# Where the operand tiles of the matmuls begin in on-chip memory, modulo 512 bytes: a two-layer decoder trunk in float32

## The chip, the core and the metric

The kernel runs on one core of a Trainium2 chip. The metric is the time of one execution on the device in microseconds (us). The kernel before took 2269.24 us in the median of three runs (2264.16 to 2272.15).

## What is computed

The reference is a decoder trunk on 256 tokens of width 2048, two layers deep, in float32, with a final RMSNorm. Cut to what matters here:

```python
h = x
# layer 0: one projection 2048 -> 6432, a gated short convolution and RWKV-7 mixing, one projection back
p = rms_norm(h, ev_norm) @ ev_w_in
mix = concat(short_conv_mixer(p[..., :3072], conv_w), rwkv7_mixer(p[..., 3072:], ...))
h = h + mix @ ev_w_out
h = h + (silu(n @ wg) * (n @ wu)) @ wd          # n = rms_norm(h, ffn_norm[0]), wg/wu 2048 x 5632
# layer 1: one projection 2048 -> 1600, a pooling mixer and 12-head latent attention, one projection back
p = rms_norm(h, od_norm) @ od_w_in
mix = concat(pool_mixer(p[..., :512], ...), mla_mixer(p[..., 512:], ...))
h = h + mix @ od_w_out
h = h + (silu(n @ wg) * (n @ wu)) @ wd          # the same block with the second set of weights
return rms_norm(h, final_norm)
```

Almost all arithmetic is in dense products of activations (256 tokens) with weights that are read once from device memory.

## The kernel before

Every dense product is done with three matmuls in a reduced float32 format (`float32r`): each operand is split into a high part and a low remainder, and high times high, high times low and low times high are summed in PSUM. Weights come in blocks of [128, 1024] through a queue of four buffers `w` (`load_next`, L67); `split_next` (L88) makes of each half a high tile `wh` (ScalarE, L96) and a low tile `wl` (VectorE, L97), [128, 512] each, six buffers of each, up to four ahead of use. One `wh` with its `wl` is a "quarter". All matmuls of the program pass through `mm` (L56), so they carry line 57 in the profile and are told apart by the names of their tiles. A name reads out <- moving operand, stationary operand: in `mm<-wh,xh` the weights stream and the activations stand.

There are two shapes of dense product. In `gemm_wt` the weights stand still (128 columns of a quarter) and 256 columns of activations stream past them. In `gemm_tok` the activations stand (128 tokens) and 512 columns of weights stream past them:

```python
# gemm_wt, L164-170: out[128 features, 256 tokens]
hi, lo = self.quarter()
for j in range(4):
    xh, xl = X[kt]
    self.mm(out, hi[:, sl], xh, kt == 0, False)
    self.mm(out, hi[:, sl], xl, False, False)
    self.mm(out, lo[:, sl], xh, False, kt == 4 * n - 1)
# gemm_tok, L181-187: out[t][128 tokens, 512 features]
for t in range(2):
    self.mm(out[t], xh[:, ts], hi, new and i == 0, False)
    self.mm(out[t], xl[:, ts], hi, False, False)
for t in range(2):
    self.mm(out[t], xh[:, ts], lo, False, stop and i == len(kts) - 1)
```

The activations are, by stage: `xh`/`xl` from `xtiles` (L141), four tiles of 4096 bytes a partition for the high and four for the low parts, used for the normed input of every projection, for the mixers' outputs in both output projections (`out_proj`, L237) and for the input of the feed-forward stages; `lh0`/`ll0` and `lh1`/`ll1` (L1108, named `lh`/`ll` in the profile), the two latents of the attention, used in `keys`, `queries` and `rotated` with `gemm_wt` and in `values` with `gemm_tok`; and `hh`/`hl` (L427), the gated hidden activations of a feed-forward stage, used in its down projections with `gemm_tok`.

The order of the stages is: the even layer's projections (`gemm_wt`, with the small matmuls of the recurrence woven between them by a list of generators, the "lane"), its output projection, feed-forward stage 0 in two halves (gate and up products of 6 blocks of 512, then the down products of these; then 5 blocks), the odd layer in the same manner, feed-forward stage 1. Nothing of this order is decided by addresses.

Where a tile begins in on-chip memory follows from the pools, which stand one behind another in every partition: `const`, then `xs` (small tiles and `xtiles`), then `wp` (`w`, `wh`, `wl`), then the pool of the running stage (`even`, `ff0`, `odd`, `ff1`). Within a pool, buffers stand in the order in which their tags are first asked for; sizes are rounded up to 32 bytes a partition. In `build`, line 305 asks for the small tags `dg`, `ssq` and `rstd` once before anything else of `xs`, and so they stand ahead of `xh` and `xl`.

Of the kernel before, what the change touches and what calls it, by code (L numbers as in the profile page):

```python
# [10 lines left out]
F32 = mybir.dt.float32  # L11
# [7 lines left out]
P = 128  # L19
# [32 lines left out]
class Trunk:  # L52
# [205 lines left out]
    def order(self):  # L258
        a, b = self.a, []
        for i in range(4):  # L260
            b.append([a["e_in"][n][:, i * 512 : i * 512 + 512] for n in range(4)])
        b += [a["e_in"][n] for n in range(4, 51)]

        def out(w, n0):
            r = [w[nb, kc] for nb in (2, 3) for kc in range(n0)]
            r += [w[nb, kc] for nb in (0, 1) for kc in range(3)]
            r += [w[nb, 3] for nb in (0, 1)]
            return r + [w[nb, kc] for nb in (2, 3) for kc in range(n0, 4)]

        def ffn(l):  # L270
            r = []
            for b0, b1 in HALVES:
                for n in range(b0, b1):
                    r += [a["f_gate"][l, n, kc] for kc in range(4)]
                    r += [a["f_up"][l, n, kc] for kc in range(4)]
                r += [a["f_down"][l, nb, kc] for nb in range(4) for kc in range(b0, b1)]
            return r

        b += out(a["e_out"], 3) + ffn(0)
        b += [a["o_in"][n] for n in range(13)]  # L280
        b += [a["w_v"][0], a["w_qp0"], a["w_kn"][0], a["w_qn"][0]]
        b += [a["w_kn"][1], a["w_qn"][1], a["w_v"][1], a["w_qp1"]]
        b += [a["w_kn"][2], a["w_qn"][2], a["w_v"][2]]
        return b + out(a["o_out"], 2) + ffn(1)

    def build(self):
        tc, nc, a = self.tc, self.nc, self.a
        self.ahead, self.half = 3, 0
        self.blocks, self.loaded, self.pend = self.order(), [], []
        self.delayed, self.lane, self.wait = [], [], 0  # L290
        with (
            tc.tile_pool(name="const", bufs=1) as cp,
            tc.tile_pool(name="xs", bufs=4) as self.xs,
            tc.tile_pool(name="wp", bufs=2) as self.wp,
            tc.tile_pool(name="psum", bufs=4, space=PSUM) as self.psum,
            tc.tile_pool(name="dram", bufs=2, space=bass.MemoryType.DRAM) as self.dp,
        ):
            self.ident = cp.tile([P, P], F32, name="ident")
            self.ones = cp.tile([P, P], F32, name="ones")
            self.pkt = cp.tile([P, NPK], F32, name="pkt")  # L300
            self.mhalf = cp.tile([P, 16], F32, name="mhalf")
            self.cos = cp.tile([P, T], F32, name="cos")
            self.sin = cp.tile([P, T], F32, name="sin")
            self.h = cp.tile([P, 2, D], F32, name="h")
            for tag, shape in (("dg", [P, P]), ("ssq", [P, 2, 4]), ("rstd", [P, 2])):
                self.xs.tile(shape, F32, tag=tag, name=tag, bufs=2)
            nc.vector.memset(self.mhalf, -0.5)
            nc.vector.memset(self.ones, 1.0)
            nc.scalar.dma_start(out=self.pkt, in_=a["pk"])
            nc.scalar.activation(self.cos[:, 0:16], self.mhalf, AF.Copy)  # L310
            with tc.tile_pool(name="even", bufs=1) as self.tp:
                X, ssq = self.even_mix()
            with tc.tile_pool(name="ff0", bufs=1) as self.tp:
                X, ssq = self.ffn(X, ssq, "g_od", self.rope_tables)
                rs = self.rstd_tok(ssq)
            with tc.tile_pool(name="odd", bufs=1) as self.tp:
                X, ssq = self.odd_mix(X, rs)
            with tc.tile_pool(name="ff1", bufs=1) as self.tp:
                self.fn = self.tp.tile([P, D], F32, tag="fn", name="fn")
                nc.gpsimd.dma_start(out=self.fn, in_=a["final_norm"].partition_broadcast(P))  # L320
                self.ffn(X, ssq, None)
# [82 lines left out]
    def ffn(self, X, ssq, gname, between=None):  # L404
        nc = self.nc
        rs = self.rstd_tok(ssq)
        new_ssq = self.xs.tile([P, 2, 4], F32, tag="ssq", name="ssq", bufs=2)
        for half, (b0, b1) in enumerate(HALVES):
            HX = []
            if half and between:  # L410
                between()
            for b in range(b0, b1):
                pg = self.gemm_tok(X, range(4))
                sg, ac = [], []
                for t in range(2):
                    s = self.tp.tile([P, 512], F32, tag="sg", name="sg", bufs=2)
                    nc.scalar.activation(s, pg[t], AF.Silu, scale=rs[:, t : t + 1])
                    sg.append(s)
                pu = self.gemm_tok(X, range(4))
                for t in range(2):  # L420
                    s = self.tp.tile([P, 512], F32, tag="ac", name="ac", bufs=2)
                    nc.vector.scalar_tensor_tensor(
                        out=s, in0=pu[t], scalar=rs[:, t : t + 1], in1=sg[t],
                        op0=ALU.mult, op1=ALU.mult,
                    )
                    ac.append(s)
                hh = self.tp.tile([P, 4, T], F32R, tag="hh", name="hh", bufs=6)  # L427
                hl = self.tp.tile([P, 4, T], F32R, tag="hl", name="hl", bufs=6)
                HX += [(hh[:, j], hl[:, j]) for j in range(4)]

                def turn(ac=ac, hh=hh, hl=hl):
                    for j in range(0, 4, 2):
                        pt = self.ps()
                        for i in range(2):
                            for t in range(2):
                                nc.tensor.transpose(  # L436
                                    pt[:, i * T + t * P : i * T + t * P + P],
                                    ac[t][:, (j + i) * P : (j + i + 1) * P], self.ident,
                                )
                        self.split(  # L440
                            (hh[:, j : j + 2], hl[:, j : j + 2]),
                            pt.rearrange("p (a t) -> p a t", a=2),
                        )

                self.later(3, turn)
            X = self.xtiles() if half and gname else X
            for nb in range(4):
                if half and not gname and nb == 3:
                    self.last(HX, b1 - b0, new_ssq)
                    break  # L450
                ps = self.gemm_tok(HX, range(b1 - b0))
                if not half:
                    self.add_h(ps, nb)
                elif gname:
                    self.finish(ps, nb, new_ssq, X, gname)
                else:
                    self.add_h(ps, nb, new_ssq)
                    hs = self.h[:, :, nb * 512 : nb * 512 + 512]
                    fs = self.fn[:, nb * 512 : nb * 512 + 512]
                    nc.vector.tensor_tensor(  # L460
                        out=hs, in0=hs, in1=fs.unsqueeze(1).to_broadcast([P, 2, 512]),
                        op=ALU.mult,
                    )
        return X, new_ssq
# [970 lines left out]
```

## Time and profile before

| | |
|---|---|
| median of 3 runs | 2269.24 us |
| the profiled execution | 2269.03 us |
| its span, first to last instruction | 2267.3 us |
| TensorE busy | 2250.6 us (99%) |
| VectorE busy | 1371.0 us (60%) |
| ScalarE busy | 1166.4 us (51%) |
| DMA, mean share of 16 engines | about a half, 179 GB/s |
| granted TensorE clock, mean | 0.997 of 2.4 GHz |

Time between the first and the last instruction is the span; 1.7 us of the execution lie around it. A matmul's busy time in the profile reaches from its start to the modelled end of its pipeline, so that the busy times of neighbours overlap: one of 512 columns stands as 389 ns, while the next one starts some 227 ns after it. What a matmul takes of the span is therefore read from the distance of two starts, which the text calls its step, and not from its duration. A window's count takes in the one or two matmuls that began before it and reach into it.

### The profile page before, as it was taken

What the parts mean: (1) busy time and instruction counts of PE and PEld (TensorE: products, weight loads), DVE (VectorE), ACT (ScalarE), POOL (GpSimd) and SP (SyncE); (2) the same over time, 40 slices, a digit from 0 to 9 for tenths busy, and PEclk for the clock granted to TensorE, in tenths of its full rate; (3) what the DMA queues carried; (4) which work ended last, traced back from release to release, by engine and by line L of the source; (5) the groups of instructions that cost most, each with busy time, mean ns of one, the idle gap of its engine ahead of it and who ended that gap; (6) DMA issues with size and microseconds to landing.
All of it is one profiled execution on the core that took longest, in us unless ns stands there. A gap on an engine that the chain in (4) does not pass through costs nothing.

```text
span 2267.3 us, 33957 instructions
## 1 busy us (share of the span) xinstructions
PE 2250.6 (99%) x12422; PEld 1921.0 (85%) x12422; DVE 1371.0 (60%) x2432; ACT 1166.4 (51%) x2085; POOL 27.1 (1%) x41
## 2 busy tenths in 40 slices
PE   9999999999999999999999999999999999999998
PEld 9999898778888888888888998788888888888886
DVE  6785477648555555555556677665555555555554
ACT  7655364546545444454555544455545444454554
POOL 0000000000000000000000000000000000000000
PEclk9999999999999999999999999999999999999999
DMA  8455235625555555555555554356555555555554
GB/s 300 134 177 166 85 132 171 196 88 185 189 191 190 192 188 194 194 187 193 188 189 190 178 171 136 117 178 208 186 194 187 189 193 193 195 187 192 188 190 154
DMA packets 124680, 405.46 MB, mean 179 GB/s; under 512 B 24896, under 2 KB 25152, under 8 KB 124128
## 3 DMA queue, kind: packets, MB, share of 16 engines
q1 hardware_dynamic: 122896, 398.31, 52.5%
q0 software_dynamic: 896, 3.80, 0.6%
q8 instruction: 97, 1.59, 0.3%
q10 hardware_dynamic: 720, 1.18, 0.1%
q14 instruction: 71, 0.58, 0.1%
HBM read 400.10 MB, written 3.15 MB: 178 GB/s over the span
## 4 chain that ended last, share of the span: by engine, by line
PE 96%; DMA 2%; DVE 1%; ACT 1%; issue 0%; SPq 0%; POOL 0%; POOLq 0%; DVEq 0%; ACTq 0%
PE mm L57 87%; PE sm L57 6%; PE sm L436 1%; DVE wl L97 1%; DMA xt<-x 0%; PE sm L198 0%; DMA Nb<-dN 0%; DMA xr<-xT 0%; DMA dN<-DG 0%; DMA pkt<-pk 0%; PE sm L1241 0%; ACT wh L96 0%; PE sm L700 0%; ACT xh L154 0%; PE sm L743 0%
## 5 line engine op out<-in xcount | busy, mean ns | idle before, releaser
L97 DVE TENSOR_TENSOR wl<-w,wh 128x512 fp32r<-128x512 f32 x1482 | 1017.3, 691 | 764.6 <-ACT wh L96 750.6
L96 ACT ACTIVATE wh<-w 128x512 fp32r<-128x512 f32 x1482 | 931.4, 631 | 952.1 <-DVE wl L97 630.1
L57 PE MATMUL mm<-wh,xh 128*128 128x512 f32 x1664 | 654.4, 393 | 2.2 <-ACT xh L151 2.2
L57 PE MATMUL mm<-wh,xl 128*128 128x512 f32 x1664 | 649.4, 390 | 1.2 <-DVE xl L152 1.2
L57 PE MATMUL mm<-wl,xh 128*128 128x512 f32 x1664 | 513.7, 390 | 0.0
L57 PEld LDWEIGHTS mm<-wh,xh 128*128 128x128 f32 x1664 | 312.9, 188 | 68.5 <-ACT xh L151 2.7
L57 PEld LDWEIGHTS mm<-wh,xl 128*128 128x128 f32 x1664 | 313.2, 188 | 64.8 <-DVE xl L152 1.5
L57 PEld LDWEIGHTS mm<-wl,xh 128*128 128x128 f32 x1664 | 312.6, 188 | 65.3
L57 PE MATMUL mm<-xh,wh 128*128 128x256 f32 x992 | 288.5, 291 | 1.3 <-ACT wh L96 1.3
L57 PE MATMUL mm<-xh,wl 128*128 128x256 f32 x992 | 282.4, 285 | 1.3 <-DVE wl L97 1.3
L57 PE MATMUL mm<-xl,wh 128*128 128x256 f32 x992 | 282.1, 284 | 0.0
L57 PE MATMUL mm<-wh,hh 128*128 128x512 f32 x704 | 274.5, 390 | 0.0
L57 PE MATMUL mm<-wh,hl 128*128 128x512 f32 x704 | 273.9, 389 | 0.0
L57 PE MATMUL mm<-wl,hh 128*128 128x512 f32 x704 | 219.9, 389 | 0.0
L57 PEld LDWEIGHTS mm<-xh,wh 128*128 128x128 f32 x992 | 190.1, 192 | 5.1 <-ACT wh L96 2.0
L57 PEld LDWEIGHTS mm<-xh,wl 128*128 128x128 f32 x992 | 189.9, 191 | 1.8 <-DVE wl L97 1.7
L57 PEld LDWEIGHTS mm<-xl,wh 128*128 128x128 f32 x992 | 190.2, 192 | 0.5
L57 PEld LDWEIGHTS mm<-wl,hh 128*128 128x128 f32 x704 | 132.2, 188 | 27.4
L57 PEld LDWEIGHTS mm<-wh,hh 128*128 128x128 f32 x704 | 132.2, 188 | 27.3
L57 PEld LDWEIGHTS mm<-wh,hl 128*128 128x128 f32 x704 | 132.2, 188 | 27.0
L228 DVE TENSOR_TENSOR h<-mm,h 128x512 f32<-128x512 f32 x54 | 34.9, 684 | 4.4 <-PE mm L57 4.3
L57 PE MATMUL mm<-lh,wh 128*128 128x256 f32 x120 | 35.4, 295 | 0.0
(256 smaller groups left out, 1279.1 us busy)
## 6 DMA issues: line engine op xcount, KB each, us to landing
w<-f_gate SPq DMA_DIRECT2D x176, 512.0 KB, 3.7
w<-f_up SPq DMA_DIRECT2D x176, 512.0 KB, 3.6
w<-f_down SPq DMA_DIRECT2D x176, 512.0 KB, 3.6
w<-e_in SPq DMA_DIRECT2D x94, 512.0 KB, 3.8
w<-e_out SPq DMA_DIRECT2D x32, 512.0 KB, 3.8
w<-o_out SPq DMA_DIRECT2D x32, 512.0 KB, 3.6
w<-o_in SPq DMA_DIRECT2D x26, 512.0 KB, 3.6
w<-e_in SPq DMA_DIRECT2D x16, 256.0 KB, 6.0
```

The costliest lines, as they stand in the source:

```text
L57: return self.nc.tensor.matmul(out, lhsT, rhs, start=start, stop=stop)
L96: nc.scalar.activation(hi, w[:, sl], AF.Copy)
L97: nc.vector.tensor_tensor(out=lo, in0=w[:, sl], in1=hi.bitcast(F32), op=ALU.subtract)
L228: nc.vector.tensor_tensor(out=hs, in0=ps[t], in1=hs, op=ALU.add)
L436: nc.tensor.transpose(pt[:, i * T + t * P : i * T + t * P + P], ac[t][:, (j + i) * P : (j + i + 1) * P], self.ident,)
```

## The change

Two tags are added and one group of tiles is asked for earlier. No instruction is added, removed or moved: the built programs have the same instructions in the same order on every engine, with the same waits. The two `gap` tiles are never written or read.

```diff
             self.h = cp.tile([P, 2, D], F32, name="h")
+            self.xtiles()
             for tag, shape in (("dg", [P, P]), ("ssq", [P, 2, 4]), ("rstd", [P, 2])):
                 self.xs.tile(shape, F32, tag=tag, name=tag, bufs=2)
+            self.xs.tile([P, 80], F32, tag="gap", name="gap", bufs=1)
...
     def ffn(self, X, ssq, gname, between=None):
         rs = self.rstd_tok(ssq)
         new_ssq = self.xs.tile([P, 2, 4], F32, tag="ssq", name="ssq", bufs=2)
+        self.tp.tile([P, 112 if gname else 8], F32, tag="gap", name="gap")
```

What that does to the addresses can be counted from the sizes. The pool `xs` begins at byte 37024 of a partition, which is 160 modulo 512. Before, `dg` (2 x 512 bytes), `ssq` and `rstd` (2 x 32 each) came first, 1152 bytes, so `xh` began at 288 modulo 512; all of `xh`, `xl`, `w`, `wh`, `wl`, `sg`, `ac`, `hh` and `hl` are multiples of 512 long, so all of these began at 288. Now `xh` and `xl` come first and begin at 160, and behind them stand the 1152 bytes and the gap of 320, so that the weights begin at 96 (160 + 1472 = 1632 = 3 x 512 + 96). In feed-forward stage 0 (`gname` is set) a gap of 448 bytes comes next, in stage 1 the 8192 bytes of `fn` and a gap of 32. The latents `lh`/`ll` stand behind 64 bytes of odd size in the odd layer's pool, before and now.

| tiles | begin modulo 512, before | now | activations minus weights, before | now |
|---|---|---|---|---|
| `wh`, `wl` | 288 | 96 | | |
| `xh`, `xl` | 288 | 160 | 0 | +64 |
| `lh`, `ll` | 352 | 160 | +64 | +64 |
| `hh`, `hl`, stage 0 | 288 | 32 | 0 | -64 |
| `hh`, `hl`, stage 1 | 288 | 128 | 0 | +32 |

Slices of these tiles start at multiples of 512 bytes from the tile's start, so the last two columns hold for every matmul of the dense products. The tiles `ident`, `ones` and `h` stay where they were; all other tiles of the even and the odd layer move together by 320 bytes.

## Rows read from the trace of the kernel before

**Rows 1.** The page: span, busy times, chain that ended last.
```profile
span 2267.3 us, 33957 instructions
...
PE 2250.6 (99%) x12422; PEld 1921.0 (85%) x12422; DVE 1371.0 (60%) x2432; ACT 1166.4 (51%) x2085; POOL 27.1 (1%) x41
...
PE 96%; DMA 2%; DVE 1%; ACT 1%; issue 0%; SPq 0%; POOL 0%; POOLq 0%; DVEq 0%; ACTq 0%
```

**Rows 2.** TensorE by tiles (names, shapes, count | busy us, mean ns | idle before).
```profile
L57 PE MATMUL mm<-wh,xh 128*128 128x512 f32 x1664 | 654.4, 393 | 2.2 <-ACT xh L151 2.2
...
L57 PE MATMUL mm<-xh,wh 128*128 128x256 f32 x992 | 288.5, 291 | 1.3 <-ACT wh L96 1.3
...
L57 PE MATMUL mm<-wh,hh 128*128 128x512 f32 x704 | 274.5, 390 | 0.0
...
L57 PE MATMUL mm<-wl,lh 128*128 128x512 f32 x24 | 7.5, 395 | 0.0
```

**Rows 3.** Windows (us, each engine's busy us (count), granted clock, DMA share, GB/s).
```profile
130.68:202.44 71.76, 71.76 (x601) 71.76 (x599) 56.70 (x139) 37.49 (x64) 0.00 (x0) 1.00 0.64 200
1357.16:1362.70 5.54, 5.54 (x50) 5.54 (x48) 4.35 (x9) 2.53 (x4) 0.00 (x0) 1.00 0.59 200
1338.53:1344.13 5.60, 5.60 (x26) 4.49 (x25) 3.54 (x6) 2.79 (x5) 0.00 (x0) 1.00 0.61 198
525.65:791.90 266.25, 266.25 (x1200) 221.06 (x1199) 159.82 (x262) 137.04 (x226) 1.32 (x2) 1.00 0.57 189
792.13:923.36 131.23, 131.23 (x585) 108.78 (x583) 72.36 (x106) 61.55 (x99) 0.00 (x0) 1.00 0.58 192
1796.28:1927.50 131.22, 131.22 (x584) 108.78 (x583) 72.35 (x106) 61.53 (x99) 0.00 (x0) 1.00 0.57 192
```

**Rows 4.** TensorE in order of time, gate and up products (start us, us, ...).
```profile
600.20 0.39 PE L57 MATMUL mm<-wh,xl 128*128 128x512 f32 x1
...
604.05 0.39 PE L57 MATMUL mm<-wh,xh 128*128 128x512 f32 x1
```

**Rows 5.** The same view, `values` of the odd layer.
```profile
1338.53 0.39 PE L57 MATMUL mm<-wh,lh 128*128 128x512 f32 x1
1338.77 0.39 PE L57 MATMUL mm<-wh,ll 128*128 128x512 f32 x1
...
1344.13 0.28 PE L57 MATMUL mm<-lh,wh 128*128 128x256 f32 x1
```

**Rows 6.** The same view, odd output projection, behind float32 transposes.
```profile
1426.20 0.40 PE L57 MATMUL mm<-wh,xl 128*128 128x512 f32 x1
1426.44 0.40 PE L57 MATMUL mm<-wh,xh 128*128 128x512 f32 x1
...
1429.31 0.39 PE L57 MATMUL mm<-wh,xl 128*128 128x512 f32 x1
...
1430.70 0.39 PE L57 MATMUL mm<-wh,xl 128*128 128x512 f32 x1
...
1431.38 0.61 PE L57 MATMUL mm<-wl,xh 128*128 128x512 f32 x2
```

**Rows 7.** TensorE by one tile: durations ns min/median/max, first and last start.
```profile
L57 PE MATMUL mm<-wh,xh x1664: 387/389/628, 393.2 to 2148.0; 128*128 128x512 f32 x185
...
L57 PE MATMUL mm<-wh,lh x24: 392/394/586, 1338.5 to 1414.5; 128*128 128x512 f32 x24
...
L436 PE MATMUL sm<-ident,ac x176: 270/272/273, 572.8 to 2152.4; 128*128 128x128 f32 x176
L198 PE MATMUL sm<-ident,h x96: 271/272/273, 509.4 to 1533.3; 128*128 128x128 f32 x96
```

**Rows 8.** Weight loads beside matmuls, gate and up products, in order of time.
```profile
600.88 0.39 PE L57 MATMUL mm<-wh,xh 128*128 128x512 f32 x1
600.88 0.19 PEld L57 LDWEIGHTS mm<-wh,xl 128*128 128x128 f32 x1
```

**Rows 9.** Waits from 526 to 1256 us (who <- for whom: us, times, longest).
```profile
ACT wh L96 <- DVE wl L97: 300.7, 413, 0.7
DVE wl L97 <- ACT wh L96: 298.2, 454, 1.0
ACT wh L96 <- PE mm L57: 50.9, 84, 0.8
```

## The prediction, made before the changed kernel had run

> **What bounds the kernel now.** I read the page's head first: TensorE is busy 99% of the span and 96% of the chain that ended last is TensorE [rows 1]. The groups by tiles show how little it waits: 2.2 us before the first activations, and nothing of size elsewhere [rows 2]. Nor do the engines that feed it press: in the first feed-forward stage the two that split the weights wait mostly for each other, and ScalarE for TensorE, 50.9 us [rows 9]. So the time is a sum of TensorE's steps, and a change counts only if it alters the distance between the starts of neighbouring matmuls. The clock can't: the windows show it granted in full (1.00, so 2.4 GHz) [rows 3].
>
> Next I read the steps, in three places where the same two loops run undisturbed.
>
> - Weights stream, 512 columns, activations start with them modulo 512 bytes (before: `xh`, `xl`, `hh`, `hl`). 17 steps from 600.20 to 604.05 us [rows 4]: 3.85 / 17 = 226.5 ns. The window of the gate and up products agrees: 1152 such matmuls and 48 transposes fill 266.25 us [rows 3]; at 226.7 and about 109 ns they give 261.2 + 5.2 = 266.4. I use 226.7.
> - The same loop with activations 64 bytes behind the weights. The kernel before has this in one place, `values` with `lh` and `ll`: 24 steps from 1338.53 to 1344.13 [rows 5], 5.60 / 24 = 233.3 ns, even from the second matmul on (1338.53 to 1338.77), and with about the same load on the other engines (ScalarE 2.79 us of 5.60, against 137.04 of 266.25 in the gate and up products) [rows 3]. The duration is longer too, 394 ns against 389 in the median [rows 7].
> - Activations stream, 256 columns. Aligned: 601 matmuls touch the window from 130.68 to 202.44, two of them from before it, so 598 steps in 71.76 us [rows 3], 120.0 ns. With `lh`, 64 bytes behind: 48 matmuls, 47 steps in 5.54 us, 117.9 ns.
>
> 512 columns at 2.4 GHz are 213.3 ns and 256 are 106.7, so both aligned steps carry 13.3 ns above the streaming, and the shifted ones 20.0 and 11.2. The weight load of the next matmul starts together with each matmul (both at 600.88 [rows 8]). I read this as two reads of the same memory running side by side: how far their starts lie apart modulo 512 decides how often one holds up the other. That reading is an inference; the steps are measured.
>
> **The change part by part.** No instruction moves, so there is no order to discuss; each family of dense matmuls gets a new distance.
>
> *Feed-forward gate and up (`xh`, `xl`, +64).* There are 3 x 1664 = 4992 `gemm_tok` matmuls on `xh`/`xl` [rows 2]. The two output projections take 2 x 384 of them (16 quarters a block, 4 blocks, 6 matmuls), the feed-forward stages 4224. They come to stand exactly as `lh` stands to the weights in `values`, so I take its step: 4224 x (233.3 - 226.7) = 4224 x 6.6 = +27.9 us. Bounds: no change at all (0), and 240 ns, the slowest regular step of an aligned matmul (1426.20 to 1426.44 [rows 6]), +56 us; below, the shortest duration is 2 ns under the median (387 against 389 [rows 7]), which gives -8.4.
>
> *Output projections (`xh`, `xl`, +64), 768 matmuls.* Here small matmuls of the lane break the run, and an aligned run needs some matmuls to settle: six steps from 1429.31 to 1430.70 take 1.39 us, 231.7 each, the next three to 1431.38 take 0.68, 226.7 each [rows 6]. With about as many of the one as of the other the mean now is some 229 (an estimate from these rows); at 233.3, 768 x 4.3 = +3.3 us.
>
> *Projections with streaming activations (`xh`, `xl`), 3072 matmuls* (51 and 13 blocks of 16 x 3; 3 x 992 of them stand under these names [rows 2]). They take the step of `lh`: 3072 x (120.0 - 117.9) = -6.5 us. Bounds: 0, as many are held up by the lane's matmuls anyway, and below twice this, -13.
>
> *Down products of stage 0 (-64), 1056 matmuls* (half of 3 x 704 [rows 2]). No 512-column row has stationary activations ahead of the weights. The nearest row in the sense of the distance is the 256-column one with `lh`, where the moving tile lies 64 behind the standing one, as it will here; it lost 2.1 ns. I take the 2 ns that the shortest duration allows: -2.1 us. Bounds: -2.2 and, at 240 ns, +14.
>
> *Down products of stage 1 (+32), 1056 matmuls.* Nothing in the trace has this distance. Halfway between 0 (226.7) and +64 (233.3) is 230.0: +3.5 us. Bounds: -2.1 and +14.
>
> *All else.* Transposes of `ac` against `ident` get other distances in both stages, but transposes from tiles at different distances (`ac`, `h`) last the same 272 ns [rows 7]: 0, at most a nanosecond or two on 176. The splits on ScalarE and VectorE keep all their tiles aligned with each other, and were they slower, their cover is the time in which they wait for each other and for TensorE [rows 9]; a slower TensorE only lengthens that. DMA at 0.57 of its engines in the long stages [rows 3] is asked for less in each microsecond, not more.
>
> Sum: +27.9 + 3.3 - 6.5 - 2.1 + 3.5 = +26.1 us on the profiled execution's 2269.03: 2295 us, 1.1% slower. That execution lies 0.2 us from the median, so the same number stands for the runs.
>
> The trace shows more than the streaming time in every step, 13.3 ns for aligned operands and 20.0 in `values` [rows 3]. The Trainium skill, TensorE: Matmul & The Clock Gate, section "Step-by-step: what each phase is for", says the opposite of my reading: the engine has two independent read ports, and loading the next tile's weights takes no bandwidth from the running matmul. By that rule no distance matters, each term is zero, and the sum is 2269 us; it is one of the rivals. The trace does not agree as far as it goes, since only the distance of the tiles is known to differ between 226.7 and 233.3 ns.
>
> **The rivals.**
>
> *Alignment is itself the collision, and any shift helps.* For it: the 256-column row, faster by 2.1 ns when shifted, and 13.3 ns of excess in each aligned step, which something must cause. Against it: `values`, slower when shifted, in all of its 24 steps. If the shifted 512-column matmuls all reached the shortest duration, (4992 + 2112) x 2 ns = -14.2, with the -6.5 of the others: 2248 us, faster. If they went down by a whole 6.6 ns, as far as `values` went up: -47 - 6.5, 2216. Since the 256-column matmuls bring the time to the edge of faster by themselves, it decides as soon as the 512-column steps don't grow.
>
> *The 233.3 belongs to the place and not to the distance.* `values` is short (24 matmuls in this run), comes right behind 256-column matmuls, and aligned matmuls behind a break also step by 231.7 for a while [rows 6]. In a long run the shifted matmuls would then settle to 226.7 as the aligned ones do. Against it: those settle after six or seven steps, the 24 show no sign of it. Then only the -6.5 remains: 2262.5 us, just at the edge of faster.
>
> *Distances do not matter.* The skill's rule as above, or that the distance that counts is not taken modulo 512 and the change so does not do what it says. For it: the long trace has only one aligned distance, so the contrast rests on the odd layer alone. 2269 us.
>
> *Both gated stages collide fully.* Nothing in the trace shows distances of -64 and +32 with 512 columns; at 240 ns each they cost +14 instead of -2.1 and +3.5: 2295 + 16 + 10.5 = 2322 us.
>
> **How the numbers follow.** I give the forecast 0.62; its own range, from gate and up at +5 ns with free gated stages (2269 + 21 - 6.5 - 2 = 2281) to one gated stage at 240 (2311), is 2281 to 2311. Collision by alignment 0.15, place not distance 0.10, no effect 0.08, both gated stages at their worst 0.05. About 0.3% (6.8 us) is what a measurement of this kernel can tell from no change. Slower: the forecast and the worst case, 0.67. Faster: the first rival and half of the second, 0.20. Same: the third and the other half, 0.13. The range of 8 in 10 leaves out the first rival and the worst case beyond 2316: 2256 to 2316.
>
> **What would show it.** In the profile of the changed kernel: steps of 233.3 ns in the windows of the gate and up products, which then last 1152 x 6.6 = 7.6 us longer in each first half (266.25 to about 274); the streaming projections at 117.9; the down products of the first halves, 576 matmuls, at 131.23 - 1.2 = 130 us in stage 0 and 131.22 + 1.9 = 133 in stage 1. The matmuls `mm<-wh,xh` should stand at 394 ns in the median. `values` must stay at 233.3, since its distance is not touched. I am wrong if the gate and up windows stay at 266 us or get shorter, or if the clock or waits of TensorE change.

## The result and the profile after

The changed kernel takes 2302.13 us in the median (2299.79 to 2311.64, 4 runs) against 2269.85 us of the kernel before on the same chip: ratio 1.0159, 95% interval 1.0134 to 1.0184. The ratio is worked out from the single runs and not from the two medians, which divide to 1.0142, inside the interval. The forecast was 2295 us.

The head of the page after: span, busy time of each engine, and the shares of the chain that ended last. To be compared with [rows 1].

```profile
span 2298.0 us, 33957 instructions
...
PE 2282.8 (99%) x12422; PEld 1914.5 (83%) x12422; DVE 1371.2 (60%) x2432; ACT 1166.9 (51%) x2085; POOL 27.2 (1%) x41
...
PE 96%; DVE 2%; DMA 1%; ACT 1%; issue 0%; POOLq 0%; POOL 0%; SPq 0%; DVEq 0%
```

The same instructions, TensorE still busy 99% of the span and 96% of the chain, and its busy time up by 32.2 us, while the other engines stand within 0.5 us of before. The time went into TensorE's own steps and not into a wait.

Windows of the kernel after (us; busy us and count of PE, PEld, DVE, ACT, POOL; granted clock; DMA share; GB/s), in this order: gate and up of stage 0's first half, its down products, `values` of the odd layer, and the down products of stage 1's first half. They answer to the last four windows of [rows 3], where `values` stands first.

```profile
519.05:792.88 273.83, 273.83 (x1200) 221.09 (x1199) 159.87 (x262) 137.15 (x226) 1.32 (x2) 1.00 0.55 184
793.11:925.61 132.50, 132.50 (x584) 108.84 (x583) 72.30 (x106) 61.52 (x99) 0.00 (x0) 1.00 0.57 190
1346.93:1352.53 5.60, 5.60 (x26) 4.52 (x25) 3.57 (x7) 2.80 (x5) 0.00 (x0) 1.00 0.62 204
1813.76:1948.79 135.03, 135.03 (x584) 108.89 (x583) 72.24 (x106) 61.61 (x99) 0.00 (x0) 1.00 0.55 186
```

Gate and up went from 266.25 to 273.83 us at the same granted clock of 1.00 and with DMA at 0.55 instead of 0.57; the down products went from 131.23 to 132.50 and from 131.22 to 135.03; `values`, whose distance the change leaves alone, stayed at 5.60. Step by step, about the same place of the gate and up loop as in [rows 4], TensorE in order of time (start us, us, engine, line):

```profile
600.61 0.40 PE L57 MATMUL mm<-wh,xh 128*128 128x512 f32 x1
...
604.34 0.39 PE L57 MATMUL mm<-wl,xh 128*128 128x512 f32 x1
```

These are 16 steps in 3.73 us, 233.1 ns each, where before 17 took 3.85 us, 226.5 each. The durations by tile (ns, min/median/max), beside [rows 7]:

```profile
L57 PE MATMUL mm<-wh,xh x1664: 390/398/632, 385.1 to 2175.6; 128*128 128x512 f32 x185
...
L57 PE MATMUL mm<-wh,hh x704: 388/395/477, 793.1 to 2288.7; 128*128 128x512 f32 x176
...
L57 PE MATMUL mm<-xh,wh x992: 276/279/468, 6.9 to 1346.6; 128*128 128x256 f32 x199
```

And the waits from 519 to 1266 us (who <- for whom: us, times, longest), beside [rows 9]:

```profile
DVE wl L97 <- ACT wh L96: 314.7, 457, 1.0
ACT wh L96 <- PE mm L57: 265.4, 360, 0.8
ACT wh L96 <- DVE wl L97: 102.3, 138, 0.7
```

A wait is put down to whoever came last. For ScalarE's splits that was TensorE for 50.9 us before and is for 265.4 now, while the part put down to VectorE fell from 300.7 to 102.3. Their sum tells more: 351.6 us before and 367.7 now, and VectorE's wait went from 298.2 to 314.7, both some 16 us more in a stretch that is 17 us longer. The engines that feed TensorE got the added time as slack, since only TensorE became slower.

The whole span can be put together from stage windows of the two traces (length in us, from the first dense matmul of a stage to the first of the next, the first stage from the start of the span):

| stage | before | after | difference | predicted |
|---|---|---|---|---|
| streaming projections, even layer | 393.22 | 385.13 | -8.1 | |
| streaming projections and attention, odd layer | 158.60 | 157.27 | -1.3 | -6.5 with the row above |
| output projections, even and odd | 246.50 | 249.63 | +3.1 | +3.3 |
| gate and up, four halves | 975.31 | 1003.06 | +27.8 | +27.9 |
| down, stage 0 | 243.82 | 246.15 | +2.3 | -2.1 |
| down, stage 1 | 240.92 | 247.89 | +7.0 | +3.5 |
| the rest | 8.9 | 8.9 | 0.0 | 0 |
| span | 2267.3 | 2298.0 | +30.7 | +26.1 |

The first row of the table as windows, before and after:

```profile
0.00:393.22 393.22, 387.19 (x3249) 366.40 (x3249) 274.08 (x623) 221.53 (x455) 15.38 (x27) 0.99 0.51 166
0.00:385.13 385.13, 380.35 (x3248) 360.75 (x3248) 274.29 (x623) 221.53 (x455) 15.39 (x27) 0.99 0.52 170
```

### The profile page after: what moved, and what is told of

Read it like the earlier page. It is cut to its first block, busy times and chain, and to the rows that moved or that the text cites. A ratio compares the mean times of both kernels' runs of the same rounds, so it can differ in the third digit from the quotient of the medians.

```text
span 2298.0 us, 33957 instructions
## 1 busy us (share of the span) xinstructions
PE 2282.8 (99%) x12422; PEld 1914.5 (83%) x12422; DVE 1371.2 (60%) x2432; ACT 1166.9 (51%) x2085; POOL 27.2 (1%) x41
## 4 chain that ended last, share of the span: by engine, by line
PE 96%; DVE 2%; DMA 1%; ACT 1%; issue 0%; POOLq 0%; POOL 0%; SPq 0%; DVEq 0%
PE mm L57 88%; PE sm L57 7%; PE sm L439 1%; DVE wl L97 1%; PE sm L198 0%; DMA Nb<-dN 0%; DMA dN<-DG 0%; DVE Tb L811 0%; DVE ou L807 0%; PE sm L1244 0%; DMA pkt<-pk 0%; ACT wh L96 0%; PE sm L703 0%; PE sm L746 0%; DVE h L607 0%
## 5 line engine op out<-in xcount | busy, mean ns | idle before, releaser
L57 PE MATMUL mm<-wh,xh 128*128 128x512 f32 x1664 | 665.9, 400 | 2.0 <-ACT xh L151 2.0
L57 PE MATMUL mm<-wh,xl 128*128 128x512 f32 x1664 | 656.7, 395 | 1.2 <-DVE xl L152 1.2
L57 PE MATMUL mm<-wl,xh 128*128 128x512 f32 x1664 | 524.0, 396 | 0.0
L57 PE MATMUL mm<-lh,wh 128*128 128x256 f32 x120 | 35.4, 295 | 0.0
```

The lines of the kernel that those rows point to most:

```text
L57: return self.nc.tensor.matmul(out, lhsT, rhs, start=start, stop=stop)
```

## The experiments

Nine kernels were run. Three of them (`e1_map`, `e5_kinds`, `e9_scan`) are small programs that only repeat matmuls of a known distance in place of the layers; the others are the kernel with tiles moved. The distance is always where the activations begin minus where the weights begin.

### `xh` and `xl` alone, and the gated activations alone

`e2_x_only` is the changed kernel with `hh` and `hl` back at distance 0:

```diff
-        self.tp.tile([P, 112 if gname else 8], F32, tag="gap", name="gap")
+        self.tp.tile([P, 128], F32, tag="gap", name="gap")
```

> The changed kernel with the gated activations brought back to distance 0 (gap of 512 bytes in both feed-forward stages), xh and xl left 64 bytes behind the weights. If every family of matmuls has its own step by its own distance: gate and up windows as in the changed kernel (273.8 us for 1152 matmuls), down products back to 131.2 for 576, and the whole 2.4 + 7.0 = 9.4 us under the changed kernel, about 2293, ratio to before 1.010. If a stage's step depends on its neighbours' distances too (the matmuls lock to one another), the down products stay above 131.2 and the ratio above 1.013.

`e3_h_only` is the kernel before with only that line of the change:

```diff
         new_ssq = self.xs.tile([P, 2, 4], F32, tag="ssq", name="ssq", bufs=2)
+        self.tp.tile([P, 112 if gname else 8], F32, tag="gap", name="gap")
```

> The kernel before with only the two gaps in the feed-forward pools: gated activations -64 and +32 from the weights, everything else at distance 0. By own distances: gate and up windows 266.25 us, down products of 576 matmuls 132.5 in stage 0 and 135.0 in stage 1, the whole +2.4 + 7.0 = 9.4 us over before, 2279, ratio 1.004. If the gated distances only cost beside shifted xh and xl: no change, ratio 1.000.

Measured: 2295.28 us for the first, ratio 1.0118 (1.0093 to 1.0142), and 2278.49 for the second, ratio 1.0045 (1.0028 to 1.0062). Against the 2269.19 of the kernel before in these rounds that is +26.1 and +9.3, 35.4 together, where the whole change measured 32.3; the intervals of the two hold the gap. The windows of gate and up and of the down products in stages 0 and 1, first of `e2_x_only`:

```profile
530.51:804.32 273.81, 273.81 (x1200) 220.31 (x1199) 159.94 (x262) 137.14 (x226) 1.32 (x2) 1.00 0.53 184
804.56:935.82 131.26, 131.26 (x585) 108.81 (x584) 72.38 (x106) 61.53 (x99) 0.00 (x0) 1.00 0.56 192
1822.38:1953.65 131.27, 131.27 (x584) 108.80 (x583) 72.39 (x106) 61.53 (x99) 0.00 (x0) 1.00 0.55 192
```

and of `e3_h_only`:

```profile
525.42:791.71 266.29, 266.29 (x1200) 221.04 (x1199) 159.91 (x262) 137.08 (x226) 1.32 (x2) 1.00 0.55 189
791.94:924.45 132.51, 132.51 (x585) 108.84 (x584) 72.39 (x106) 61.48 (x99) 0.00 (x0) 1.00 0.55 190
1798.55:1933.58 135.03, 135.03 (x585) 108.88 (x583) 72.39 (x106) 61.56 (x99) 0.00 (x0) 1.00 0.53 187
```

Each of these families follows its own distance and no other: gate and up are slow only where `xh` is shifted (273.81), the down products only where `hh` is (132.51 and 135.03).

### All tiles moved, the distances kept

`e4_all_96` is the kernel before with 96 bytes ahead of the tiles of the layers, so that weights and activations both begin at other addresses and all distances stay:

```diff
+            self.xs.tile([P, 24], F32, tag="gap", name="gap", bufs=1)
```

> The kernel before with 96 bytes ahead of all of the pool's tiles: xh, xl, w, wh, wl, hh, hl all begin at 384 modulo 512 instead of 288, every distance stays as before (0, and +64 for the latents). Distance theory: no change, steps 226.7 and 120.0, ratio 1.000 within 0.3%. Rival (absolute start against 64 or 512 bytes decides): another step in all dense matmuls, 7104 x 6.6 ns = 47 us either way.

Measured: 2266.98 us, ratio 0.9994 (0.9981 to 1.0007). Its gate and up window:

```profile
523.18:789.52 266.34, 266.34 (x1201) 221.02 (x1200) 159.98 (x262) 137.06 (x226) 1.32 (x2) 1.00 0.55 189
```

266.34 us against 266.25 before: the address itself does not matter here, the distance does.

### A map of the distances

`e1_map` runs 48 matmuls for each distance, in steps of 16 bytes, with nothing at work beside TensorE. The operands are 4-byte tiles (`float32r`, as in the kernel), filled once:

```python
group("t" + c, 512, 4 * k, 0)        # the standing tile begins 16 k bytes behind
group("w" + c, 256, 0, 4 * k)        # the streaming tile begins 16 k bytes behind
group("s" + c, 512, 16 * k, 16 * k)  # both 64 k bytes further on
```

> Not the trunk: a small program with matmuls alone, which computes nothing of the reference (its output is a copy of x). Groups of 48 matmuls in the reduced float32 format with nothing else running, four float32 transposes ahead of each. In the groups ta to tF 512 columns stream and the 128 standing columns begin 0, 16, 32 ... 496 bytes behind the streaming ones modulo 512; in wa to wF 256 columns stream and begin 0 to 496 bytes behind the standing ones; in sa to sh both are moved together by 0, 64 ... 448 bytes. Theory (the distance between the two reads sets the step): steps settle to 226.7 ns at 0 (ta), about 233.3 at +32 and +64 (tc, te), 228.9 at -64 (tC), 120.0 in wa and 117.9 in we, and all of sa to sh settle to 226.7. Rival (the step depends on the place in the program, that is on the other engines' work beside it): all groups of one shape have the same step. Rival (the absolute start decides): sa to sh differ among each other by the 7 ns that ta and te do.

Measured, the settled step in ns, from the last 24 steps of each group:

| distance, bytes | 0 | 16 | 32 | 48 | 64 | 80 | 96 | 112 | 128 | 144 | 160 | 176 | 192 | 208 | 224 | 240 |
|---|---|---|---|---|---|---|---|---|---|---|---|---|---|---|---|---|
| 512 columns | 226.7 | 226.7 | 233.3 | 233.3 | 233.3 | 232.1 | 234.2 | 233.3 | 233.3 | 233.3 | 233.3 | 230.0 | 228.9 | 233.3 | 233.3 | 228.3 |
| 256 columns | 120.0 | 116.7 | 116.7 | 118.3 | 117.8 | 120.0 | 120.0 | 113.3 | 118.7 | 118.7 | 118.8 | 119.3 | 113.3 | 119.2 | 118.3 | 117.0 |

From 256 bytes on both rows repeat themselves: the distance counts modulo 256 and not modulo 512. All eight groups with both tiles moved stand at 226.7. So both rivals fall. Windows of 24 steps each; the first seven with 512 columns at 0, 16, 32, 64, 192, 256 and 448 (that is -64 modulo 512), then four with 256 columns at 0, 64, 112 and 192, then the first group with both moved:

```profile
28.21:33.65 5.44, 5.44 (x26) 4.50 (x24) 0.00 (x0) 0.00 (x0) 0.00 (x0) 1.00 0.00 0
39.09:44.53 5.44, 5.44 (x26) 4.51 (x24) 0.00 (x0) 0.00 (x0) 0.00 (x0) 1.00 0.00 0
50.56:56.16 5.60, 5.60 (x25) 4.51 (x24) 0.00 (x0) 0.00 (x0) 0.00 (x0) 1.00 0.01 3
73.83:79.43 5.60, 5.60 (x26) 4.51 (x25) 0.00 (x0) 0.00 (x0) 0.00 (x0) 1.00 0.00 0
166.67:172.16 5.49, 5.49 (x26) 4.51 (x24) 0.00 (x0) 0.00 (x0) 0.00 (x0) 1.00 0.01 3
212.75:218.19 5.44, 5.44 (x26) 4.51 (x24) 0.00 (x0) 0.00 (x0) 0.00 (x0) 1.00 0.00 0
351.95:357.45 5.50, 5.50 (x26) 4.51 (x25) 0.00 (x0) 0.00 (x0) 0.00 (x0) 1.00 0.00 0
395.55:398.43 2.88, 2.88 (x27) 2.88 (x25) 0.00 (x0) 0.00 (x0) 0.00 (x0) 1.00 0.02 6
419.90:422.73 2.83, 2.83 (x27) 2.83 (x25) 0.00 (x0) 0.00 (x0) 0.00 (x0) 1.00 0.00 0
438.34:441.06 2.72, 2.72 (x27) 2.72 (x25) 0.00 (x0) 0.00 (x0) 0.00 (x0) 1.00 0.02 6
468.82:471.55 2.73, 2.73 (x27) 2.73 (x25) 0.00 (x0) 0.00 (x0) 0.00 (x0) 1.00 0.02 6
593.33:598.77 5.44, 5.44 (x26) 4.50 (x24) 0.00 (x0) 0.00 (x0) 0.00 (x0) 1.00 0.00 0
```

5.44 / 24 is 226.7, 5.60 / 24 is 233.3, 5.49 to 5.50 is 228.9. These are the kernel's own steps in the three shifted families: 233.3 at +64, 233.3 at +32, 228.9 at -64. Since VectorE, ScalarE and GpSimd stand at 0.00 here, no traffic of other engines is needed for it. The map holds one run of 48 matmuls for each distance; that a distance can have a second step is shown further on.

### Which part of the load counts

`e5_kinds` repeats 512-column matmuls at distances 0, 64 and 160 with standing tiles of 128, 96, 64 and 32 columns, and then with 2-byte operands at 0, 32, 64, 160 and 192:

```python
for c, wide in (("full", 128), ("most", 96), ("half", 64), ("few", 32)):
    for e, d in (("Z", 0), ("L", 64), ("M", 160)):
        last = group(c + e, d, wide)
```

> The small program again (nothing of the reference is computed), 512 streaming columns, 48 matmuls a group. full/most/half/few: 128, 96, 64 and 32 standing columns, each at 0 (Z), +64 (L) and +160 (M) bytes; bf: both operands in bfloat16 at 0, 32, 64, 160 and 192 bytes. Theory (the weight load and the streaming read of the same memory hold each other up while both run): the excess over 213.3 ns falls with fewer standing columns, the differences between Z, L and M shrink with it, and with 32 columns all lie within 3 ns of each other; in bfloat16, with half the bytes read, the pattern of distances is another and the excess smaller. Rival (a fixed cost of starting at given addresses, paid once per matmul whatever is read after): Z 226.7, L and M 233.3 for all four widths.

| ns for a step | 0 | 64 | 160 |
|---|---|---|---|
| 128 columns standing | 226.7 | 233.3 | 233.3 |
| 96 | 230.0 | 233.3 | 233.3 |
| 64 | 230.0 | 232.75 | 231.1 |
| 32 | 231.7 | 231.1 | 233.2 |
| 2-byte operands, 128 columns | 215.8 | 215.8 | 215.8 |

Windows of 24 steps: 128 columns at 64, 64 columns at 0, 32 columns at 0 and at 64, and the 2-byte operands at 0:

```profile
38.65:44.25 5.60, 5.60 (x25) 4.51 (x24) 0.00 (x0) 0.00 (x0) 0.00 (x0) 1.00 0.00 0
96.60:102.12 5.52, 5.52 (x25) 3.22 (x24) 0.00 (x0) 0.00 (x0) 0.00 (x0) 1.00 0.00 0
131.25:136.81 5.56, 5.56 (x26) 2.62 (x25) 0.00 (x0) 0.00 (x0) 0.00 (x0) 1.00 0.00 0
142.80:148.35 5.55, 5.55 (x26) 2.59 (x25) 0.00 (x0) 0.00 (x0) 0.00 (x0) 1.00 0.00 0
165.60:170.78 5.18, 5.18 (x26) 2.35 (x24) 0.00 (x0) 0.00 (x0) 0.00 (x0) 1.00 0.01 3
```

The time of the streaming alone can be estimated from the map: at distance 0 the step of 512 columns is 226.7 - 120.0 = 106.7 ns longer than that of 256, which makes 213.3 ns for 512. The loads do get shorter (4.51 us of weight-load time in a window at full width, 2.6 at 32 columns), but the excess over these 213.3 ns does not: with the narrower loads it is 17 to 20 ns. So the account in which the excess is the time that two reads run side by side missed. Its other part came true: the spread between distances shrinks with the load, 6.7, 3.3, 2.75 and 2.1 ns. But that is not because the slow ones become as fast as the aligned one (they lose 2.2 ns at most); the aligned one becomes slow, by 5 ns. The rival of a fixed cost for each start missed too, as the aligned step grows when the load gets shorter. With 2-byte operands the five distances give one step. What remains is that distance counts for `float32r` operands, most of all with a full-width load, and that the aligned case is one favourable state; what inside the machine makes the state is open.

### The modulus, in the kernel

`e6_mod256` is the changed kernel with gaps that put `xh`, `xl` and stage 0's `hh` at 256 from the weights and stage 1's `hh` at 128:

```diff
-            self.xs.tile([P, 80], F32, tag="gap", name="gap", bufs=1)
+            self.xs.tile([P, 32], F32, tag="gap", name="gap", bufs=1)
...
-        self.tp.tile([P, 112 if gname else 8], F32, tag="gap", name="gap")
+        self.tp.tile([P, 64 if gname else 32], F32, tag="gap", name="gap")
```

> The trunk with xh and xl 256 bytes from the weights, gated activations at +256 in stage 0 and +128 in stage 1. The small program repeats itself after 256 bytes. If that holds in the trunk: gate and up windows 266.3 us and streaming projections 120.0 as before, stage 0 down products 131.2, stage 1 down products at 233.3 a step, 135.0; the whole +7 us, ratio 1.003. If the modulus is 512, xh and xl at 256 cost like a distance the aligned case does not know: gate and up windows at 270 us or more, ratio over 1.008.

Measured: 2272.82 us, ratio 1.0028 (1.0012 to 1.0044). Gate and up, and the down products of stages 0 and 1:

```profile
523.14:789.43 266.29, 266.29 (x1200) 221.00 (x1199) 159.89 (x262) 137.04 (x226) 1.32 (x2) 1.00 0.55 189
789.66:920.90 131.24, 131.24 (x585) 108.75 (x583) 72.36 (x106) 61.56 (x99) 0.00 (x0) 1.00 0.55 192
1793.98:1928.48 134.50, 134.50 (x584) 109.16 (x583) 72.33 (x106) 61.54 (x99) 0.00 (x0) 1.00 0.54 188
```

At 256 these stages are as at 0; at 128 the down products step by 232.4 ns, 1 ns under the 233.3 of the map and of the forecast. Why they are 1 ns shorter here is open.

### Shifting only what streams

If the distance is free to choose, each use can have its best: 0 where the weights stream, 112 or 192 where the activations stream. `e7_best192` gives the two sets of activations that stream (the even layer's input and what stage 0 hands to the odd layer) 192 bytes and leaves the others at 0; `sumsq`'s scratch shares a buffer to make room, and the latents move to +192:

```diff
-    def xtiles(self):
-        xh = [self.xs.tile([P, 4, T], F32R, tag="xh", name="xh") for _ in range(4)]
...
+    def xtiles(self, sh=0):
+        def four(tag):
+            ts = [self.xs.tile([P, 4 * T + 64], F32R, tag=tag, name=tag) for _ in range(4)]
+            return [
+                t[:, sh : sh + 4 * T].rearrange("p (a t) -> p a t", a=4) for t in ts
...
-            X = self.xtiles() if half and gname else X
+            X = self.xtiles(48) if half and gname else X
...
-        X = self.xtiles()
+        X = self.xtiles(48)
...
+        tp.tile([P, 32], F32, name="gap")
```

> The kernel before with each family at its own best distance: xh and xl at 0 where they stand (output projections, feed-forward), at +192 where they stream (the inputs of both layers' projections; the tiles are 256 bytes longer and a view begins 192 bytes into them), latents at +192; the scratch of the sums of squares shares a buffer in the even layer to make room. By the small program: streaming projections settle to 113.3 ns in place of 120.0, 3072 x 6.7 = -20.5 us if every run settled, about -15 with the lane breaking runs; latents -1.9 us; everything else as before. Ratio 0.992 to 0.994. If addresses only trade places with other limits (the splits on ScalarE and VectorE, the DMA queue) the streaming stages do not get shorter: 1.000.

`e8_best112` is the same with `xtiles(28)`, 112 bytes; its latents too stand at +192.

> As e7 with the streaming xh and xl at +112 instead of +192. The small program has the same settled 113.3 ns there, but takes 11 matmuls to settle in place of 5: -12 us and -1.9, ratio 0.994, a little behind e7.

Measured: 2252.92 us, ratio 0.9933 (0.9919 to 0.9947), and 2251.73 us, ratio 0.9923 (0.991 to 0.9935). Both beat the kernel before, the first by as much as forecast; I had put the second a little behind the first, and they came out level. In `e7_best192` the odd layer's projections show two states of one distance (TensorE in order of time):

```profile
1252.95 0.28 PE L57 MATMUL mm<-xl,wh 128*128 128x256 f32 x1
...
1271.65 0.28 PE L57 MATMUL mm<-xl,wh 128*128 128x256 f32 x1
...
1271.88 1.84 PE L57 MATMUL sm<-ones,lq 128*128 128x1 f32 x16
...
1279.89 0.28 PE L57 MATMUL mm<-xl,wh 128*128 128x256 f32 x1
...
1296.49 0.28 PE L57 MATMUL mm<-xl,wh 128*128 128x256 f32 x1
```

55 times three matmuls take 18.70 us from 1252.95 to 1271.65, 113.3 ns each. Then small matmuls break the run twice, at 1271.88 and at 1276.49, and behind them, with the same tiles at the same distance, 47 times three take 16.60 us, 117.7 each. In `e8_best112` the run goes back to 113.3 behind these breaks. Its even stage of projections and the odd layer's run as windows:

```profile
0.00:379.26 379.26, 374.14 (x3249) 353.56 (x3249) 273.39 (x623) 220.63 (x455) 15.37 (x27) 1.00 0.51 173
...
1244.63:1322.34 77.71, 77.65 (x678) 77.26 (x677) 52.52 (x104) 43.80 (x85) 4.39 (x6) 1.00 0.52 182
```

The odd run, all 624 matmuls of these projections, takes 77.71 us there, 79.28 in `e7_best192`, 81.28 in the kernel before; the even stage takes 379.26 and 379.30, where the aligned tiles took 390.2 to 393.2 in four traces.

Two states are not a property of 192 bytes alone. In `e2_x_only` the activations stream at +64, and the same place of the odd run, up to the same small matmuls, looks so:

```profile
1282.74 0.28 PE L57 MATMUL mm<-xh,wh 128*128 128x256 f32 x1
...
1302.12 0.28 PE L57 MATMUL mm<-xh,wh 128*128 128x256 f32 x1
```

57 times three matmuls in 19.38 us are 113.3 ns each, and behind the small matmuls the step is 117.8 again; in the changed kernel, at the same +64, the whole odd run steps by 117.8, the breaks apart. So the odd run of `e2_x_only` takes 79.28 us, the same as at +192. What the distance changes is how often each state is met: of 2256 stretches of three successive steps in the even stage, 1879 stand within half a nanosecond of 117.8 and 87 of 113.3 in the changed kernel (+64), 187 and 1827 in `e7_best192` (+192). With 512 columns it happens too: the 24 steps of `values`, at +192 in both kernels, take 5.60 us in `e7_best192` and 5.50 in `e8_best112`, 233.3 and 229.2 ns each:

```profile
1324.81:1330.41 5.60, 5.60 (x26) 4.54 (x25) 3.56 (x7) 2.80 (x5) 0.00 (x0) 1.00 0.60 203
1322.46:1327.96 5.50, 5.50 (x27) 4.51 (x25) 3.62 (x7) 2.79 (x5) 0.00 (x0) 1.00 0.63 205
```

What decides between the states is open.

### A better mix for the rest

`e9_scan` runs the gate and up loop (two quarters of `xh`, `xl` against high and low weights) for 512 mixes of distances of `xh`, `xl` and the low weights, each from 0 to 224 in steps of 32:

```python
nc.tensor.matmul(t[k], xh[k], hi, start=i == 0, stop=False)
nc.tensor.matmul(t[k], xl[k], hi, start=False, stop=False)
...
nc.tensor.matmul(t[k], xh[k], lo, start=False, stop=i == n - 1)
```

> The small program (nothing of the reference is computed) with the six matmuls of gemm_tok in their order: xh and xl standing against the streaming high weights, xh against the low ones, six rounds a group. The three distances are set apart: xh at 0, 32 ... 224 bytes from the high weights (second letter of the group's name, a to h), xl likewise (third letter), the low weights likewise (fourth letter), 512 groups. If a step is set by each matmul and its neighbours' own distances alone, no mix is under the aligned group gaaa, 226.7 ns, and most are at 229 to 234. Rival (mixed distances can lock the sequence at a shorter step, as the 256-column matmuls do at +112 and +192, 113.3 instead of 120.0): some group settles near 220.0 ns, which would be worth 7104 x 6.7 = 47 us in the trunk.

Measured: the mix with all at 0 is the shortest, 226.7 ns, and no other reaches it; seven follow at 228.9, the median of all is 232.2, the longest 238.9. Windows of 18 steps: all at 0, two of the 228.9, and the longest:

```profile
24.28:28.36 4.08, 4.08 (x20) 3.38 (x18) 0.00 (x0) 0.00 (x0) 0.00 (x0) 1.00 0.01 4
173.24:177.36 4.12, 4.12 (x19) 3.38 (x18) 0.00 (x0) 0.00 (x0) 0.00 (x0) 1.00 0.00 0
3821.99:3826.11 4.12, 4.12 (x19) 3.38 (x18) 0.00 (x0) 0.00 (x0) 0.00 (x0) 1.00 0.02 4
1887.13:1891.43 4.30, 4.30 (x20) 3.40 (x18) 0.00 (x0) 0.00 (x0) 0.00 (x0) 1.00 0.00 0
```

Each mix was met once, for 36 matmuls. As far as that shows, nothing is left to win there by a gap of a multiple of 32 bytes: the kernel before already had the best distance where the weights stream.

## Why the prediction was right

*What bounds the kernel.* Right: only TensorE's steps changed. The mean granted clock was 0.997 before and 0.996 after, the splits take as long as before, and the engines that feed TensorE only wait longer.

*Gate and up.* Right in mechanism and size: +27.8 us of stage time against +27.9. One place of 24 matmuls in the kernel before, `values`, was enough, because its distance was the very one that the change was to make and its step even from the second matmul on. That one place speaks for thousands of matmuls was not certain, as `values` at +192 shows with its two steps; at +64 with 512 columns the gate and up products step by 233.3 in both traces that have them there. The sign to look for was the step; the median duration of `mm<-wh,xh`, which I had put at 394 ns, is 398.

*Output projections.* +3.1 against +3.3. Over the steps under 260 ns the mean is 233.2 there, against 228.3 to 228.9 in traces with aligned tiles; the forecast had 233.3 and some 229.

*Streaming projections.* -9.4 between the two profiles against -6.5. The odd run steps by 118 as forecast, and its stage gave 1.3 us for 624 matmuls, 2.1 ns each; that is the more common of two states at this distance, which the forecast did not know of. The even stage gave 8.1 where the term had 2448 x 2.1 = 5.1. Its steps under 160 ns average 119.9 in all four aligned traces and 117.6 and 117.5 in the two shifted ones, 2.3 ns less or 5.6 us for 2448, so the size of a step was nearly right. The length of this stage also differs between traces of the same distances: aligned it is 393.22 us in the kernel before, and 390.21, 390.70 and 390.81 in `e3_h_only`, `e4_all_96` and `e6_mod256`; shifted 385.13 after and 388.37 in `e2_x_only`. The means, 391.2 and 386.7, lie 4.5 apart, and the other 3.6 are which two traces were compared.

*Down products of stage 0.* This is the step that failed, in sign. I took the 256-column row of `lh` as the nearest and 2 ns less for each matmul, -2.1 us; at -64 they step by 228.9, which is 2.2 more, +2.3 us. `e3_h_only` shows it with nothing else changed and `e1_map` with nothing else running. What was wrong was to carry a gain from the loop in which the activations stream to the one in which they stand: the map's two rows have different minima (0 and 16 against 112 and 192), so a step of the one row can't be read off the other.

*Down products of stage 1.* Right in sign, half in size: +7.0 against +3.5. I took a step halfway between those of 0 and +64, as if it grew with the distance. It doesn't: 16 bytes cost nothing and 32 cost all of it (226.7, 233.3). The bound of 240 ns held.

*The sum.* 2295 against 2302: of the 7 us between them, 4.4 and 3.5 come from the two down terms, the projections gave 2.9 back, and the profiled execution, 2299.79 us, lies 2.3 below the median of the runs. That the projections took back part of what the down terms lacked is luck.

*The reading.* That the step follows how far their starts lie apart is shown, by moving both operands (nothing changes) or one (the step does). It does not follow from that alone, as the two states of one distance show. The modulus is 256 and not 512, which made no difference to the forecast, since +64, -64 and +32 are distinct in both. "Two reads that hold each other up while both run" is not shown: with a load a quarter as wide, the excess stayed.

The Trainium skill, TensorE: Matmul & The Clock Gate, section "Step-by-step: what each phase is for", has the load and the stream on independent read ports, so that loading takes nothing from the running matmul. For 2-byte operands the runs agree as far as distance goes: 215.8 ns at five distances. For `float32r` operands they do not agree: 226.7 or 233.3 with nothing but the distance changed.

The Trainium skill, TensorE: Matmul & The Clock Gate, section "Back-to-back issue gap", gives 2.5 ns above the streaming time for an isolated matmul, which makes 215.8 at 512 columns, and about 131 ns for a sustained stream of loads and matmuls. The 2-byte groups, with a load for each matmul, agree with the first figure; no run here shows the second.

*The rivals.* "Any shift helps" falls with gate and up at 273.83. "The place and not the distance" falls with 233.3 kept through 1152 matmuls and with `e4_all_96`. "Distances do not matter" falls with `e2_x_only` and `e3_h_only`. "Both gated stages collide fully" was put at 240 ns; stage 1 came to 233.3 and stage 0 to 228.9.

## What to carry to other kernels

When TensorE is the bound and its operands are 4 bytes wide (`float32r`, the only such format tried), read the step between starts and not the duration, and count where each operand begins modulo 256 before a pool is reordered: a small tile put ahead of a big one cost some 1.5% here. Keep activations that stand in the array at the distance of the streaming weights (0, or 16 bytes, which only the small program tried), and give activations that stream a distance of their own (112 or 192 bytes here, 0.7 and 0.8% faster); a tile used both ways has to be decided by the larger of its uses. Take a price only from a row with the same operand in the same role, and don't interpolate between two distances: a small program that repeats one matmul at each distance measures them all in one run, though only in the state that each run happens to settle in, so a gain has to be confirmed in the kernel.

## What the runs showed of the hardware

- The step of a `float32r` matmul depends on the distance of its operands' starts modulo 256 bytes: 226.7 to 234.2 ns with 512 columns, 113.3 to 120.0 with 256 (`e1_map`). The dependence is jagged, in both roles.
- The shortest and the longest settled step of 256 columns (113.3 and 120.0) and the two most common ones of 512 (226.7 and 233.3) lie 6.7 ns apart, which is the time of 16 columns at the 106.7 ns for 256 worked out above, 64 bytes of the streaming tile. Other means are not made up of these: at 192 bytes and 512 columns the single steps of `e1_map` repeat about 226, 229 and 232 ns, 228.9 in the mean.
- One distance can have two settled states: with 256 columns 113.3 ns up to a break by small matmuls and 117.7 or 117.8 behind it, at 192 bytes (`e7_best192`) and at 64 (`e2_x_only`), each held for over a hundred steps.
- A narrower load does not make the matmul beside it faster: with 32 standing columns the aligned step is 231.7 ns, with 128 it is 226.7.
